# Attention with bias on one core: V loaded in place, late k side by side, 25 VectorE exponentials

## The chip, the cores and the metric

The kernel runs on one core of one Trainium2 chip. The core has five engines that work side by side: TensorE (PE in the profile) multiplies matrices into the score banks of PSUM, ScalarE (ACT) applies functions such as the exponential, VectorE (DVE) does elementwise work, GpSimd (POOL) and SyncE (SP) here mostly issue DMAs. Data comes from HBM into SBUF by DMA. The metric is the device time in microseconds of one execution; lower is better.

## The reference

Four batches of eight heads, 1024 queries and keys, head size 64, and one bias matrix for all heads:

```python
scale = 1.0 / np.sqrt(head_dim)
scores = scale * np.matmul(q, k.transpose(0, 1, 3, 2))
scores = scores + bias
scores_max = np.max(scores, axis=-1, keepdims=True)
attn = np.exp(scores - scores_max) / (np.sum(np.exp(scores - scores_max), axis=-1, keepdims=True) + 1e-8)
return np.matmul(attn, v).astype(np.float32)
```

All inputs and the output are float32. The kernel computes with bfloat16 operands and leaves out the maximum, which cancels in the quotient, and the 1e-8.

## The kernel before

The 32 heads are 16 pairs. The 1024 queries of a head are 8 chunks of 128, so there are 32 x 8 = 256 units of work, called slots: one head, one chunk of 128 queries against all 1024 keys. The scores of a slot lie in PSUM as 128 x 1024 numbers, keys along the partitions, in one of three places (two banks each, `places`).

A slot goes through these steps:

- **Fill** (`fill`, L254): eight matmuls add the scores of the slot to its place. A place keeps the bias of one chunk and goes from head to head: the operands hold the new head and the negated one before it, so that one fill takes the old scores out and puts the new ones in. Only where a place changes its chunk is the bias put in anew (`fill_half` with "b", L251).
- **Exponential** (`exp`, L268): one ScalarE activation from the place into a tile of `ep` (a ring of `NE` = 16 tiles E). The slots named in `PLAN` (23 of them) are left to VectorE, in five steps (`d_steps`, L285 to L301): `fixed` turns the scores into fixed point and so frees the place, `frac`, `inner`, `outer` and `last` make a polynomial of the fraction and write the bits of a bfloat16 number.
- **Attention step** (`av`, L318): eight matmuls multiply the E tile with V. V stands in `vall`, a ring of `VR` = 20 heads, 64 columns and a column of ones, so the row sum comes out as a 65th column. Up to seven slots share one bank.
- **Evacuation** (`evac`): VectorE takes the reciprocal of the sums (L326) and multiplies (L328) into one of three output tiles (`op`), and SyncE stores them, one DMA for each run of chunks of the same head (L739).

What feeds them: q and k of a pair are loaded by GpSimd, which also turns them to bfloat16, are transposed by TensorE (L191 with both heads side by side in 128 columns, L195 in two halves of 64 rows with `tile_position`), copied out of PSUM by VectorE (L203, L205) and doubled, for pairs from 7 on by DMAs that SyncE issues (L565). `EARLY` = 7: pairs 7 to 15 are the late ones. Their q is loaded side by side already (`beside`, L142: two DMAs of 64 numbers a run), their k as one DMA (L149) and transposed in halves. V is loaded into a landing tile (L169) and copied by VectorE into `vall` (L508). GpSimd holds its loads back: before it issues one, a copy of one number (`tick`, L483) waits until the load that stands `LATE` = 2 places before has landed.

The heads run in two groups, of 7 pairs (slots 0 to 111) and of 9 (112 to 255). In each group all heads go through three chunks, then the middle ones, then the last three, so all operands of the second group must be there between slot 112 and slot 160.

The order is written by a planner in the kernel's own Python, which runs at build time. It keeps a clock for each engine, with costs and latencies as constants (`FILL`, `BIAS`, `AV`, `EXP`, `ISSUE`, `DUE`, `LATER` and others), and picks the next instruction of each engine by due times. Two tables, `TURNS` and `D_TURNS`, overrule single decisions of TensorE and VectorE by their number. What it emits is a fixed order for each engine; on the chip, semaphores make each instruction wait for what it needs. So a late instruction holds up everything behind it on its engine.

Of the kernel before, what the change touches and what calls it, by code (L numbers as in the profile page):

```python
# [16 lines left out]
def kernel(  # L17
# [13 lines left out]
    nc = tc.nc  # L31
# [19 lines left out]
    NE = 16  # L51
# [11 lines left out]
    op = ctx.enter_context(tc.tile_pool(name="op", bufs=3))  # L63
# [20 lines left out]
    VR = 20  # L84
# [38 lines left out]
    for s, x in enumerate(slots):  # L123
# [5 lines left out]
    PLAN = (46, 52, 56, 73, 84, 87, 97, 107, 120, 128, 137, 149, 160, 167, 170, 182, 188, 194, 208, 214, 226,  # L129
            230, 240)  # L130
# [4 lines left out]
    BESIDE = (0,)  # L135
# [31 lines left out]
    def load_v(pr):  # L167
        lands[pr, "v"] = vland.tile([P, 2, NCH, D], BF, name="v16")
# [152 lines left out]
    def evac(b):  # L321
# [5 lines left out]
        ob = olast if n == 1 else op.tile([P, 7, D], F32, name="ob")  # L327
        nc.vector.tensor_tensor(ob[:, :n, :], po[:, :n, :D], rs[:, :n, :].to_broadcast([P, n, D]), op=ALU.mult)  # L328
        stores = []

        j = 0
        while j < n:
            x, c, h, start = slots[units[j]]
            i = j + 1
            while i < n and slots[units[i]][1:3] == (c + i - j, h):
                i += 1
            stores.append((of[:, h, c:c + i - j, :], ob[:, j:i, :]))
            j = i
        return stores

    with tc.manual_schedule():
# [10 lines left out]
        nc.vector.memset(sgn[D:, :], 1.0)  # L352
        nc.scalar.activation(warm[:], warm[:], ACTF.Exp)
# [19 lines left out]
        nc.vector.memset(vall[:, :, :, D:D1], 1.0)  # L373
# [65 lines left out]
        LATE, QCOST = 2, 4400  # L439
# [11 lines left out]
        LATER = 1500  # L451
# [3 lines left out]
        WINDOW = 4  # L455
# [22 lines left out]
        def issue(at, cost, depth, load, pr, *a):  # L478
# [6 lines left out]
            at = pool(at, 750)  # L485
# [4 lines left out]
        def load(pr, t):  # L490
            raw_at[pr, 1, 0] = issue(t, 1600, LATE, load_k, pr) + LATER
            raw_at[pr, 0, 0] = issue(t, QCOST, LATE, load_q, pr, slice(0, NCH)) + LATER
            for p in [pr - 1] * (pr > EARLY) + [pr] * (pr + 1 == NP):
                loads_v.append(p)
            next_v(t)

        def next_v(t):

            while loads_v and not any(x[2] // 2 == loads_v[0] - VR // 2 and y not in av_done for y, x in enumerate(slots)):
                if loads_v[0] - VL not in v_at:  # L500
                    break
                p = loads_v.pop(0)
                vland_at[p] = issue(t, 1600, LATE + (p > 12), load_v, p) + 2000
                move_v(p)

        def move_v(pr):
            def run(t2):
# [4 lines left out]

# [215 lines left out]
        def close(b, tag, t):  # L728
            units = bank[b][1]
            cost = 230 + 80 + 65 * len(units)  # L730
            last = len(av_done) >= NS - 1
# [176 lines left out]
```

## Time and profile before

| | |
|---|---|
| three runs | 230.94, 232.37, 232.49 us, median 232.37 |
| the profiled execution | 231.17 us, its span 229.2 us |
| busy share of the span: TensorE, ScalarE, VectorE, GpSimd | 96%, 95%, 86%, 28% |
| exponentials on ScalarE, slots on VectorE | 234 instructions (two of them halves), 23 |
| stores of the output, issued by SyncE | 156, and 2 by ScalarE |
| DMA packets, of these under 512 bytes | 57373, 34864 |

The span is what the profile covers; the time of the same execution also has what lies around it. The busy time of TensorE is that of pipelined matmuls with modelled ends and does not mean that it is at its peak. ScalarE's instructions overlap in part, so the time from start to start tells more than the mean duration.

### The profile page before, as it was taken

The numbers are of one execution on the slowest core, as the hardware profiler recorded it, in microseconds if no ns is written. First come the engines' busy times: TensorE is split into PE (matmuls) and PEld (weight loads), VectorE is DVE, ScalarE is ACT, GpSimd is POOL, SyncE is SP. The second block draws the span as 40 slices with busy tenths as digits, with TensorE's granted clock in tenths as the row PEclk, the third lists the DMA queues.
The fourth block names the chain that finished last, engine by engine and source line by source line (L and its number), as shares of the span: only waits on it lengthen the run. The fifth ranks groups of instructions, "written<-read, shape, count | busy, mean of one in ns | idle before, by whom it ended". The sixth has DMA issues, their size and how long they took to land.

```text
span 229.2 us, 10571 instructions
## 1 busy us (share of the span) xinstructions
PE 219.4 (96%) x4607; PEld 208.8 (91%) x4607; DVE 197.0 (86%) x301; ACT 218.1 (95%) x238; POOL 65.1 (28%) x115
## 2 busy tenths in 40 slices
PE   7899989999999999999999999999999999899992
PEld 2789989999999999999899999999999999899991
DVE  2578878629977999999999999999999999999952
ACT  3699999999999999999999999999999999999992
POOL 8816466256455443443224310000000000000000
PEclk9999999999999999999999999999999999999998
DMA  6999999989999999999899994111121102311122
GB/s 195 216 204 215 227 227 186 223 118 110 135 113 179 169 159 184 179 97 178 207 163 243 169 238 113 49 43 43 43 50 39 44 9 66 82 50 40 34 77 75
DMA packets 57373, 29.75 MB, mean 130 GB/s; under 512 B 34864, under 2 KB 53680, under 8 KB 57328
## 3 DMA queue, kind: packets, MB, share of 16 engines
q0 software_dynamic: 30336, 14.06, 49.3%
q1 hardware_dynamic: 26560, 14.40, 23.2%
q8 instruction: 36, 0.59, 1.1%
q10 hardware_dynamic: 432, 0.62, 0.9%
q14 instruction: 9, 0.07, 0.1%
HBM read 29.36 MB, written 8.39 MB: 165 GB/s over the span
## 4 chain that ended last, share of the span: by engine, by line
PE 54%; ACT 14%; DVE 12%; issue 7%; DMA 5%; SPq 5%; DVEq 0%; ACTq 0%
PE pl L254 31%; PE po L318 16%; ACT E L268 14%; SPq L739 5%; DMA out_dram<-ob 3%; PE px L191 3%; PE pl L251 2%; PE px L195 2%; DVE dy L285 2%; DMA df<-in_k_dram 2%; DVE ob L328 2%; DVE df L296 1%; DVE de L301 1%; DVE ko L203 1%; DVE side L222 1%
## 5 line engine op out<-in xcount | busy, mean ns | idle before, releaser
L268 ACT ACTIVATE E<-pl 128x1024 bf16<-128x1024 f32 (+1 forms) x234 | 215.0, 1094 | 2.3 <-PE pl L254 2.0
L318 PE MATMUL po<-vall,E 128*128 128x65 bf16 x1864 | 86.2, 194 | 1.1 <-DVE qo L205 0.4
L254 PE MATMUL pl<-qo,ko 128*128 128x128 bf16 x1024 | 77.0, 219 | 1.2 <-ACT E L268 0.6
L318 PEld LDWEIGHTS <-E 128*128 128x128 bf16 x1864 | 74.0, 98 | 2.0 <-DVE ob L328 0.6
L254 PEld LDWEIGHTS <-ko 128*128 128x128 bf16 x1160 | 69.4, 98 | 4.3 <-issue 1.4
L254 PE MATMUL pl<-qe,ke 128*128 128x128 bf16 x888 | 65.4, 219 | 0.9 <-ACT E L268 0.3
L254 PEld LDWEIGHTS <-ke 128*128 128x128 bf16 x888 | 53.2, 98 | 2.6 <-issue 0.7
L285 DVE TENSOR_SCALAR dy<-pl 128x1024 int32<-128x1024 f32 x23 | 28.0, 1218 | 1.8 <-PE pl L254 1.7
L301 DVE SCALAR_TENSOR_TENSOR de<-dy,df 128x1024 uint16<-128x1024 int32 x23 | 27.9, 1219 | 0.7 <-PE po L318 0.4
L296 DVE SCALAR_TENSOR_TENSOR df<-df 128x1024 f32<-128x1024 f32 x23 | 28.0, 1217 | 0.1
L293 DVE SCALAR_TENSOR_TENSOR df<-df 128x1024 f32<-128x1024 f32 x23 | 27.9, 1217 | 0.1
L328 DVE TENSOR_TENSOR ob<-po,rs 128x448 f32<-128x448 f32 (+4 forms) x40 | 23.3, 583 | 2.6 <-DMA out_dram<-ob 1.1
L142 POOL DMA_DIRECT2D q<-in_q_dram x18 | 16.3, 907 | 4.4 <-PE pl L254 2.7
L326 DVE RECIPROCAL rs<-po 128x7 f32<-128x7 f32 (+5 forms) x41 | 7.9, 192 | 9.9 <-PE po L318 9.8
L290 DVE TENSOR_SCALAR df<-dy 128x1024 f32<-128x1024 uint16 x23 | 15.8, 687 | 0.3
L483 POOL COPY tick<-q 1x1 bf16<-1x1 bf16 x12 | 4.4, 367 | 33.4 <-DMA q<-in_q_dram 33.4
L203 DVE COPY ko<-px 128x1024 bf16<-128x1024 bf16 (+1 forms) x16 | 10.7, 668 | 3.3 <-PE px L195 2.5
L205 DVE TENSOR_SCALAR qo<-px,sgn 128x1024 bf16<-128x1024 bf16 (+2 forms) x18 | 12.3, 683 | 1.2 <-PE px L191 1.0
L169 POOL DMA_DIRECT2D v<-in_v_dram x16 | 11.3, 707 | 2.0 <-DVE df L296 0.3
L251 PE MATMUL pl<-ident,braw 128*128 128x128 bf16 x136 | 11.3, 226 | 0.0
L149 POOL DMA_DIRECT2D k<-in_k_dram x15 | 10.7, 711 | 2.1 <-issue 0.8
L251 PEld LDWEIGHTS <-braw 128*128 128x128 bf16 x136 | 9.9, 148 | 0.0
(58 smaller groups left out, 125.4 us busy)
## 6 DMA issues: line engine op xcount, KB each, us to landing
v<-in_v_dram POOLq DMA_DIRECT2D x16, 256.0 KB, 6.6
k<-in_k_dram POOLq DMA_DIRECT2D x15, 256.0 KB, 5.5
out_dram<-ob SPq DMA_DIRECT2D x33, 96.0 KB, 3.9
out_dram<-ob SPq DMA_DIRECT2D x92, 32.0 KB, 2.6
ke<-ko SPq DMA_DIRECT2D x22, 128.0 KB, 5.5
q<-in_q_dram POOLq DMA_DIRECT2D x18, 128.0 KB, 4.7
qe<-q SPq DMA_DIRECT2D x17, 128.0 KB, 5.0
out_dram<-ob SPq DMA_DIRECT2D x31, 64.0 KB, 2.7
```

Source lines behind the costliest of these rows:

```text
L142: nc.gpsimd.dma_start(out=t[:, :, y, :], in_=(qf, kf)[x][pr][:, y].rearrange("p (c d) -> p c d", d=D))
L203: nc.vector.tensor_copy(t["ko"][:, cs, :], px[:])
L251: nc.tensor.matmul(to, braw[:, c, :].rearrange("p (kp kc) -> p kc kp", kc=NCH)[:, kc, :], ident8[:], start=i == 0, stop=False, skip_group_ ...
L254: nc.tensor.matmul(to, kk[:, kc, :], qq[:, c, :], start=False, stop=True, skip_group_check=True)
L268: nc.scalar.activation(e[:, i:i + n].rearrange("p b x -> p (b x)"), places[slots[s][0]][:, i:i + n].rearrange("p b x -> p (b x)"), ACTF.Ex ...
L285: w.tensor_scalar(t["y"][:], places[slots[s][0]].rearrange("p b x -> p (b x)"), scale * LOG2E * 65536.0, 127.0 * 65536.0, op0=ALU.mult, op ...
L290: w.tensor_scalar(t["f"][:], t["lo"], GU / 65536.0, None, op0=ALU.mult)
L293: w.scalar_tensor_tensor(t["f"][:], t["f"][:], GP, t["f"][:], op0=ALU.add, op1=ALU.mult)
L296: w.scalar_tensor_tensor(t["f"][:], t["f"][:], GQ, t["f"][:], op0=ALU.add, op1=ALU.mult)
L301: w.scalar_tensor_tensor(etile[s].bitcast(U16).rearrange("p c q -> p (c q)"), t["y"][:], 1.0 / 512.0, t["f"][:], op0=ALU.mult, op1=ALU.add)
L318: nc.tensor.matmul(po[:, j + i, :], etile[s][:, kc, :], vall[:, slots[s][2] % VR, kc, :], start=j + i + kc == 0, stop=kc == NCH - 1, skip_ ...
L328: nc.vector.tensor_tensor(ob[:, :n, :], po[:, :n, :D], rs[:, :n, :].to_broadcast([P, n, D]), op=ALU.mult)
```

## The change

- `VR` goes from 20 to 24 heads, and V of the pairs from 7 on is loaded straight into `vall` by two DMAs, one for each head, without a landing tile and without VectorE's copy.
- k of the late pairs is loaded side by side, as q is, and transposed in eight whole pieces.
- Three late loads may be in flight instead of two (`LATE`).
- 25 slots go to VectorE instead of 23, at other places (`PLAN`); the ring of E tiles has 13 tiles instead of 16.
- Stores are joined: chunks of one head or heads of one chunk at an even distance go out in one DMA (`joined`), 133 in all. There are four output tiles; only an evacuation of one unit that is closed last of all uses `olast`.
- The memset of V's ones stands earlier at the start.
- The planner has other constants, and both tables of turns are empty.

```diff
-    NE = 16
+    NE = 13
-    op = ctx.enter_context(tc.tile_pool(name="op", bufs=3))
+    op = ctx.enter_context(tc.tile_pool(name="op", bufs=4))
-    VR = 20
+    VR = 24
-    PLAN = (46, 52, 56, 73, 84, 87, 97, 107, 120, 128, 137, 149, 160, 167, 170, 182, 188, 194, 208, 214, 226,
-            230, 240)
+    PLAN = (42, 46, 54, 72, 74, 83, 90, 97, 107, 112, 135, 138, 151, 158, 161, 173, 180, 186, 194, 207, 213,
+            217, 228, 238, 246)
-    BESIDE = (0,)
+    BESIDE, INPLACE = (0, 1), 7
     def load_v(pr):
+        if pr >= INPLACE:
+            for t in range(2):
+                nc.gpsimd.dma_start(out=vall[:, (2 * pr + t) % VR, :, :D], in_=vf[pr][:, t])
+            return vall[:1, (2 * pr + 1) % VR, NCH - 1, D - 1:D]
...
+    def joined(units):
+
+        out, left = [], list(range(len(units)))
+        while left:
+            best = left[:1]
+            for j in left[1:]:
+                run, dj = [left[0], j], j - left[0]
+                dc, dh = (units[j][i] - units[left[0]][i] for i in range(2))
+                if min(dc, dh) < 0 or dc and dh:
+                    continue
+                while run[-1] + dj in left and units[run[-1] + dj] == (units[run[-1]][0] + dc, units[run[-1]][1] + dh):
+                    run.append(run[-1] + dj)
+                best = max(best, run, key=len)
+            left = [j for j in left if j not in best]
...
-    def evac(b):
+    def evac(b, last):
...
-        ob = olast if n == 1 else op.tile([P, 7, D], F32, name="ob")
+        ob = olast if n == 1 and last else op.tile([P, 7, D], F32, name="ob")
...
+        return [(to, ob[:, js]) for to, js in joined([slots[u][1:3] for u in units])]
...
+        nc.vector.memset(vall[:, :, :, D:D1], 1.0)
         nc.scalar.activation(warm[:], warm[:], ACTF.Exp)
...
-        FILL, BIAS, AV = 452, 500, 264
+        FILL, BIAS, AV = 452, 530, 264
-        ISSUE, COPY = 70, 7000
+        ISSUE, COPY = 420, 7000
-        DUE = (78, 86, 137, 98, 82, 97, 114, 84, 144)
-        t_pe, t_act, t_dve, t_pool = 9300.0, 9900.0, 9600.0, 9000
-        filled, used = {0: T0}, {0: 9900 + L_ACT}
+        DUE = (56, 89, 71, 156, 50, 70, 141, 54, 56)
+        t_pe, t_act, t_dve, t_pool = 9050.0, 9740.0, 9600.0, 9000
+        filled, used = {0: T0}, {0: 9740 + L_ACT}
-        LATE, QCOST = 2, 4400
+        LATE, COSTS = 3, {"k": 2300, "q": 2300, "v": 2300}
-        LATER = 1500
+        LATER = 1000
-        WINDOW = 4
+        WINDOW, GRACE = 4, 16
...
-            at = pool(at, 750)
+            two = pr >= EARLY and load in [load_q] * (0 in BESIDE) + [load_k] * (1 in BESIDE) or load is load_v and pr >= INPLACE
+            at = pool(at, 1500 if two else 750)
...
         def move_v(pr):
+            if pr >= INPLACE:
+                v_at[pr] = vland_at[pr] + 300
+                return
...
-            ok = [x for x in others if x[0] + x[1] <= limit]
+            ok = [x for x in others if x[0] + x[1] <= limit + GRACE]
...
-        TURNS = {9: 2, 15: 0, 25: 1, 30: 0, 49: 2, 63: 2, 64: 0, 74: 1, 93: 0, 94: 0, 98: 0, 105: 0, 109: 0,
...
-        D_TURNS = {1: 0, 25: 0, 34: 1, 39: 2, 41: 1, 42: 1, 44: 1, 66: 0, 68: 0, 70: 1, 71: 0, 76: 1, 81: 1,
...
+        TURNS = {}
+        D_TURNS = {}
```

More of the change, by code (lines that the diff above doesn't have):

```diff
@@ L490, in load @@
         def load(pr, t):
-            raw_at[pr, 1, 0] = issue(t, 1600, LATE, load_k, pr) + LATER
-            raw_at[pr, 0, 0] = issue(t, QCOST, LATE, load_q, pr, slice(0, NCH)) + LATER
+            raw_at[pr, 1, 0] = issue(t, COSTS["k"], LATE, load_k, pr) + LATER
+            raw_at[pr, 0, 0] = issue(t, COSTS["q"], LATE, load_q, pr, slice(0, NCH)) + LATER
             for p in [pr - 1] * (pr > EARLY) + [pr] * (pr + 1 == NP):
@@ L730, in close @@
             cost = 230 + 80 + 65 * len(units)
-            last = len(av_done) >= NS - 1
+            last, whole = len(av_done) >= NS - 1, len(av_done) == NS
             def run(t2):
-                stores = evac(b)
+                stores = evac(b, whole)
                 for i, (to, of_) in enumerate(stores):
```

22 lines of the change are left out of this document (7 added, 15 removed), and 3 rows, old and new, of the table TURNS.

## The prediction

> **What bounds the kernel now.** I read the busy times first, then ScalarE's timeline, because the busy times name three candidates at once:
>
> ```profile
> span 229.2 us, 10571 instructions
> ...
> PE 219.4 (96%) x4607; PEld 208.8 (91%) x4607; DVE 197.0 (86%) x301; ACT 218.1 (95%) x238; POOL 65.1 (28%) x115
> ...
> 8.22 0.60 ACT L268 ACTIVATE E<-pl 128x512 bf16<-128x512 f32 x1 [0.79 <-PE pl L254]
> ...
> 10.69 15.70 ACT L268 ACTIVATE E<-pl 128x1024 bf16<-128x1024 f32 x17
> ...
> 25.16 1.22 ACT L268 ACTIVATE E<-pl 128x1024 bf16<-128x1024 f32 x1
> ...
> 223.47 1.22 ACT L268 ACTIVATE E<-pl 128x1024 bf16<-128x1024 f32 x1
> ```
>
> The last four rows are ScalarE's timeline: start, time taken, instruction, count. The run of 17 exponentials that starts at 10.69 ends with the one at 25.16, so one starts every (25.16 - 10.69) / 16 = 0.904 us, although each lasts longer: they overlap. There are 234 (232 whole, two halves). From the one at 25.16 to the last there are 214 steps: 214 x 0.904 = 193.5 us at best, 223.47 - 25.16 = 198.3 us in fact. So ScalarE is never idle for long, and its hesitations from there on come to **4.9 us**. The last exponential ends at 223.47 + 1.22 = 224.7; 4.5 us of tail follow. The number of exponentials sets the time; all else can only add to those 4.9 us or take from them.
>
> Who makes it hesitate is read later in the run, where the other engines have no room either:
>
> ```profile
> 100.00:120.00 20.00, 19.80 (x410) 18.58 (x407) 19.01 (x28) 20.00 (x23) 5.03 (x9) 1.00 0.99 170
> 120.00:140.00 20.00, 19.90 (x435) 19.27 (x433) 19.53 (x31) 20.00 (x23) 6.18 (x11) 1.00 1.09 210
> 140.00:160.00 20.00, 19.89 (x431) 19.59 (x429) 19.66 (x25) 19.85 (x22) 0.00 (x0) 1.00 0.18 48
> ...
> sum 120.00, PE 118.41 PEld 114.70 DVE 116.15 ACT 119.75 POOL 11.21; mean PE 19.74 PEld 19.12 DVE 19.36 ACT 19.96 POOL 1.87
> ```
>
> These are busy times by stage (matmuls, weight loads, VectorE, ScalarE, GpSimd; then the granted clock, 1.00 throughout, and the DMA columns); the sum covers 100 to 220 us. VectorE is busy for 116.15 of 120 us there: 3.85 us idle. The page's 86% hides that, since it averages in a start with little VectorE work.
>
> **The change, part by part.**
>
> *25 VectorE slots in place of 23.* Two exponentials leave ScalarE: 2 x 0.904 = **-1.8 us** on the path. VectorE pays for it, with a chain of five steps a slot:
>
> ```profile
> 203.16 1.21 DVE L285 TENSOR_SCALAR dy<-pl 128x1024 int32<-128x1024 f32 x1
> 204.29 1.22 DVE L293 SCALAR_TENSOR_TENSOR df<-df 128x1024 f32<-128x1024 f32 x1
> 205.43 0.69 DVE L290 TENSOR_SCALAR df<-dy 128x1024 f32<-128x1024 uint16 x1
> 206.03 1.22 DVE L296 SCALAR_TENSOR_TENSOR df<-df 128x1024 f32<-128x1024 f32 x1
> 207.16 1.22 DVE L293 SCALAR_TENSOR_TENSOR df<-df 128x1024 f32<-128x1024 f32 x1
> ```
>
> Back to back they start 1.13, 1.14, 0.60 and 1.13 us apart, and the fifth kind (the one that writes `de`) I take at 1.13 too: 5.13 us a slot, 10.3 us for two.
>
> *V of nine late pairs in place; the tail.* In place, nine copies go:
>
> ```profile
> L508 DVE COPY vall<-v 128x1024 bf16<-128x1024 bf16 x16 | 6.9, 433 | 0.8 <-DMA v<-in_v_dram 0.8
> ...
> L203 DVE COPY ko<-px 128x1024 bf16<-128x1024 bf16 (+1 forms) x16 | 10.7, 668 | 3.3 <-PE px L195 2.5
> ...
> L228 DVE TENSOR_SCALAR q<-qo x9: 416/428/852, 69.6 to 136.9; 128x1024 bf16<-128x1024 bf16 x9
> ...
> 224.75 0.43 PE L318 MATMUL po<-vall,E 128*128 128x65 bf16 x8 [0.33 <-ACT E L268]
> ...
> 225.69 0.29 DVE L328 TENSOR_TENSOR ob<-po,rs 128x128 f32<-128x128 f32 x1 [1.06 <-DMA out_dram<-ob]
> 225.90 0.16 DVE L326 RECIPROCAL rs<-po 128x1 f32<-128x1 f32 x1
> 226.09 0.23 DVE L328 TENSOR_TENSOR olast<-po,rs 128x64 f32<-128x64 f32 x1
> ```
>
> That is 9 x 0.433 = 3.9 us of VectorE, so the engine's total grows by 6.4 us, but not evenly. Counted in the built order behind the hundredth exponential, the change has one 0.60 and three 1.13 steps more (+4.0 us), two evacuations with five units more (0.33 us each and 0.06 a unit by the last rows: +1.0), six copies of V fewer (-2.6), one copy at 0.67 and one negation at 0.43 fewer (-1.1): **+1.3 us where 3.85 are free**, in a stretch that should be 1.8 us shorter. 3.85 - 1.3 - 1.8 = 0.75 us of idle would be left. In the sum I take this at nothing; the other bound is the first rival, and past it the second.
>
> The last rows are the tail: VectorE waited 1.06 us for a store to give back one of three output tiles. With four tiles that wait goes. What is late next is the last unit's matmuls, done at 224.75 + 0.43 = 225.18, where its reciprocal started at 225.90: of the 1.06 us the path gets about **-0.6 us**. The other bound is +1: the last VectorE slot moves from 240 to 246, six slots nearer to the end, its chain (5.1 us) and an evacuation of its own (0.39 by the last two rows) then stand among the last nine exponentials (8.1 us) with five other evacuations. I keep -0.6, since the order ends the chain before the last exponential's matmuls.
>
> *k side by side.* From the chain of waits in order of time (start, time, what):
>
> ```profile
> 24.71 0.46 PE px L191 x8
> ...
> 71.84 0.52 PE po L318 x16
> ...
> 97.20 0.57 PE px L195 x16
> 97.77 0.55 PE pl L254 x8
> ...
> 98.58 0.46 PE pl L254 x8
> ...
> 148.62 0.50 PE pl L251 x8
> ```
>
> Sixteen 64-row transposes take 0.57 us and the fill behind them 0.55 where others take 0.46; eight whole ones take 0.46. That is 0.20 us a pair, 1.8 us of TensorE for nine. Does ScalarE get it? Between the 40th and the 80th exponential, the densest part of TensorE's order, stand before: 46 fills (0.46), 43 attention steps (0.26), 7 bias sets (0.50), four transposes (two at 0.66 with the slow fill, two at 0.46): 38.1 us. After: 46 fills, 45 steps, 7 bias sets, four transposes at 0.46: 38.2. ScalarE has 40 x 0.904 = 36.2. TensorE stays overbooked by 2 us, its relief spent on steps moved forward: I take nothing for it, between -1.8 and +2.
>
> *The loads.* A k or V load becomes two, with 2,048 runs of 64 numbers where 256 runs of 512 stood:
>
> ```profile
> L142 POOL DMA_DIRECT2D q<-in_q_dram x18 | 16.3, 907 | 4.4 <-PE pl L254 2.7
> ...
> L149 POOL DMA_DIRECT2D k<-in_k_dram x15 | 10.7, 711 | 2.1 <-issue 0.8
> ...
> v<-in_v_dram POOLq DMA_DIRECT2D x16, 256.0 KB, 6.6
> k<-in_k_dram POOLq DMA_DIRECT2D x15, 256.0 KB, 5.5
> ...
> q<-in_q_dram POOLq DMA_DIRECT2D x18, 128.0 KB, 4.7
> ```
>
> GpSimd's queue: 18 x (2 x 0.907 - 0.711) = +19.9 us, where it was busy 5.03 and 6.18 us of 20 and nothing is left to load at 140. Landing: q's pair, already side by side, is down 0.907 + 4.7 = 5.6 us after its first issue, k's one load after 5.5. With three in flight instead of two I take nothing. [...]
>
> GpSimd's added issues could also hold up VectorE: the negation's row above has a median of 428 ns and a longest of 852. If all nine took the longest: 9 x 0.42 = 3.8 us of VectorE; I go by the median, nothing. [...]
>
> The parts that I cost at nothing rest on these rows, of the list of waits and of VectorE's timeline:
>
> ```profile
> DVE ob L328 <- DMA out_dram<-ob: 1.1, 1, 1.1
> ...
> 1.93 0.19 DVE L373 MEMSET vall<- 128x160 bf16 x1 [0.64 <-issue]
> ...
> 5.51 0.50 DVE L376 CAST de<-dy 128x384 bf16<-128x384 f32 x1 [2.24 <-DMA dy<-in_q_dram]
> ```
>
> *Without cost:* the joined stores (133 for 158) leave SyncE's queue sooner, and the tail's is the only wait for a store in that list. 13 tiles for E instead of 16: in ten places an attention step stands within two TensorE items of the fill whose exponential needs its tile, in eleven before; if cover fails there, each costs a pair of steps, 0.52 us. The memset of V's ones moves ahead by 0.19 us of work, into the time in which VectorE waits for q. The emptied lists of turns move everything a little; only the counts above say how.
>
> **Sum:** -1.8 - 0.6 = -2.4 us. The profiled execution took 231.17 us (span 229.2 and 2.0 around it): 228.8. The median of the three runs, 232.37, lies 1.2 higher and would give 230.0. I forecast **229.5**, its own range 228 to 231.
>
> **The rivals.**
>
> *VectorE becomes the bound, the gain is given back.* If it can't work with less idle than its 3.85 us, the stretch is 1.3 us longer instead of 1.8 shorter; with the tail 231.17 + 1.3 - 0.6 = 231.9, by the median some 232.5: no change. For it: 116.15 of 120. Against: its steps can wait, only the first of a chain holds a score bank.
>
> *Slower: the first step comes late.* Until a slot's first step (L285) has read its bank, TensorE can't fill it, and ScalarE lives on two of three. It decides once VectorE's 0.75 us are used up: the first step then finds a 1.22 us step running and waits half of it. 16 late slots x 0.61 = 9.8 us: 228.8 + 9.8 = 238.6; if half of it is covered by the other banks, 233.7. I set it at 236. For it: the first steps stand in a new order throughout. Against: today's waits of this kind are inside the 4.9 us.
>
> *The late loads are late.* A load late by its 5.6 us at the second group's start stops TensorE's fixed order: 228.8 + 5.6 = 234.4. Against: of GpSimd's idle time most was spent on the landing of q, which two loads in flight enforce and three relax:
>
> ```profile
> L483 POOL COPY tick<-q 1x1 bf16<-1x1 bf16 x12 | 4.4, 367 | 33.4 <-DMA q<-in_q_dram 33.4
> ```
>
> *Faster:* the new order halves the 4.9 us: 228.8 - 2.4 = 226.4. For it: shorter transposes, no V copies that hold up a first step.
>
> **How the numbers follow.** Forecast 0.38; gain given back 0.22; slower 0.20; late loads 0.05; faster still 0.15. One per cent, 2.3 us, is what a measurement of this kernel can tell from no change: faster is below 230.0, slower above 234.7. Seven tenths of the forecast's range lie below 230.0: 0.27 + 0.15 = 0.42. Same: 0.11 + 0.22 = 0.33. Slower: 0.25. The range goes from just below the faster case, 225.5, to the slower one, 236.
>
> **What would show it.** Right: 232 exponentials 0.904 us apart, hesitations near 4.9 us, no VectorE wait for a store at the end, VectorE busy 98 to 99% from 100 to 220. The first rival shows in hesitations near 7 us with VectorE full; the second in ScalarE waiting for fills whose bank a late first step held; the third in TensorE idle before a k or q transpose, or a V step, released by a DMA. I am wrong if hesitations grow by over 2 us, or vanish.

## The result, and the profile after

The changed kernel takes 230.33 us (median of 20 runs, 229.04 to 232.64) against 232.15 us for the kernel before, measured beside it (20 runs, 230.94 to 233.52). The ratio is 0.9927, with a 95% interval of 0.9904 to 0.9951. That is 1.8 us faster by the medians and 0.7% by the ratio, which by the bound of the prediction is "within 1%", and inside the range that it gave for its own forecast (228 to 231).

The profiled execution of the changed kernel took 232.22 us, 1.9 above its median; that of the kernel before took 231.17, 1.0 below its own. So these two profiles side by side show the change as 1.1 us slower. Kept in mind, that is no obstacle: one learns from it which part of the time varies. Here is the page of the changed kernel, the row of ScalarE's exponentials (busy us, mean ns of one, idle us before them and what ended it) and three of the load rows (KB each, median us to landing) included:

```profile
span 230.4 us, 10433 instructions
...
PE 219.2 (95%) x4535; PEld 208.9 (91%) x4535; DVE 204.0 (89%) x304; ACT 216.8 (94%) x236; POOL 82.2 (36%) x133
...
DMA packets 91437, 29.74 MB, mean 129 GB/s; under 512 B 74560, under 2 KB 87744, under 8 KB 91392
...
L272 ACT ACTIVATE E<-pl 128x1024 bf16<-128x1024 f32 (+1 forms) x232 | 213.6, 1089 | 5.6 <-PE pl L258 5.5
...
k<-in_k_dram POOLq DMA_DIRECT2D x18, 128.0 KB, 5.9
q<-in_q_dram POOLq DMA_DIRECT2D x18, 128.0 KB, 6.7
vall<-in_v_dram POOLq DMA_DIRECT2D x18, 128.0 KB, 6.0
```

232 exponentials instead of 234; 74,560 packets under 512 bytes instead of 34,864. ScalarE's timeline (start, time taken, instruction, count) gives the account by the prediction's method:

```profile
24.43 2.12 ACT L272 ACTIVATE E<-pl 128x1024 bf16<-128x1024 f32 x2
...
224.48 2.06 ACT L272 ACTIVATE E<-pl 128x1024 bf16<-128x1024 f32 x2
```

Each row is two exponentials, so between the first of the one row and the first of the other lie 212 steps: 212 x 0.904 = 191.65 us at best, 224.48 - 24.43 = 200.05 in fact. The hesitations are **8.4 us**, where they were 4.9. With the same count for all profiles, in us (the start is the time at which the 20th exponential begins, the tail what follows the start of the last one):

| profile | start | steps x 0.904 | hesitations | tail | span |
|---|---|---|---|---|---|
| before | 25.16 | 193.46 | 4.86 | 5.72 | 229.2 |
| changed | 25.34 | 191.65 | 8.40 | 5.02 | 230.4 |
| changed, second profile (first experiment) | 24.97 | 191.65 | 7.02 | 5.06 | 228.7 |

Exponentials -1.8, tail -0.7, hesitations +2.2 to +3.5 (the tail is good to 0.05 us, as the span is given in tenths). By stretches, the hesitations between 40 and 80 us are 0.71 before, 2.22 and 3.54 in the two profiles after; between 80 and 110 us 0.95, then 3.14 and 0.99; behind that 2.24, then 2.68 and 2.06. All but 0.4 us of the loss lies before 110 us.

Two kinds of places make it up. The first, in TensorE's timeline (the last bracket is its idle time before the row and what ended it), and in the chain of waits:

```profile
93.64 0.44 PE L258 MATMUL pl<-qo,ko 128*128 128x128 bf16 x5 [1.52 <-issue]
...
100.66 0.58 PE L322 MATMUL po<-vall,E 128*128 128x65 bf16 x13 [1.16 <-issue]
```

```profile
91.94 0.18 PE pl L258 x3
92.12 1.52 issue
93.64 0.44 PE pl L258 x5
```

TensorE stops in the middle of a group of eight matmuls, after three of them, for 1.52 us; nothing that the profile shows released it. The second is a wait that can be read in ScalarE's and TensorE's timelines:

```profile
48.13 1.98 ACT L272 ACTIVATE E<-pl 128x1024 bf16<-128x1024 f32 x2 [0.44 <-PE pl L258]
```

```profile
45.95 0.69 PE L255 MATMUL pl<-ident,braw 128*128 128x128 bf16 x8
46.48 0.61 PE L258 MATMUL pl<-qz,ko 128*128 128x128 bf16 x8
46.92 0.67 PE L255 MATMUL pl<-ident,braw 128*128 128x128 bf16 x8
47.43 0.61 PE L258 MATMUL pl<-qz,ko 128*128 128x128 bf16 x8
```

The rows L255 put the bias in anew, eight matmuls more for a fill. Slots 42, 43 and 44 all carry bias and stand one behind the other, and slot 42 is now VectorE's: TensorE spends the time from 45.95 to 46.92 on a slot that gives ScalarE nothing, and ScalarE is dry at 48.13.

The other rows that the prediction named, in the views by stretch and of waits:

```profile
100.00:220.00 120.00, 117.42 (x2503) 114.58 (x2503) 115.65 (x149) 118.35 (x130) 14.67 (x20) 1.00 0.57 87
```

```profile
PEld L258 <- issue: 3.7, 9, 1.6
...
PE po L322 <- issue: 1.2, 1, 1.2
```

VectorE (the third time) is busy 115.65 of 120 us: 4.35 idle, not full. No row of the list has VectorE wait for a store. What it does have are weight loads and matmuls released by "issue", by nothing visible: the longest 1.6 and 1.5 us, where the kernel before has weight loads alone, the longest 0.7.

### The profile page after: what moved, and what is told of

Its sections match the earlier page's. It is cut to its first block, busy times and chain, and to the rows that moved or that the text cites. A ratio compares the mean times of both kernels' runs of the same rounds, so it can differ in the third digit from the quotient of the medians.

```text
span 230.4 us, 10433 instructions
## 1 busy us (share of the span) xinstructions
PE 219.2 (95%) x4535; PEld 208.9 (91%) x4535; DVE 204.0 (89%) x304; ACT 216.8 (94%) x236; POOL 82.2 (36%) x133
## 2 busy tenths in 40 slices
DMA packets 91437, 29.74 MB, mean 129 GB/s; under 512 B 74560, under 2 KB 87744, under 8 KB 91392
## 4 chain that ended last, share of the span: by engine, by line
PE 59%; ACT 19%; issue 9%; DVE 6%; DMA 3%; POOL 1%; SPq 1%; POOLq 0%; ACTq 0%
PE pl L258 34%; ACT E L272 19%; PE po L322 18%; PE px L195 4%; DMA braw<-in_bias_dram 3%; PE pl L255 2%; DVE dy L289 2%; PE px L199 1%; DVE ob L352 1%; DMA out_dram<-ob 1%; DVE df L297 1%; SPq L757 1%; POOL qz L371 0%; POOL qs L372 0%; DVE ke L218 0%
## 5 line engine op out<-in xcount | busy, mean ns | idle before, releaser
L322 PE MATMUL po<-vall,E 128*128 128x65 bf16 x1848 | 87.5, 194 | 2.0 <-issue 1.2
L258 PE MATMUL pl<-qo,ko 128*128 128x128 bf16 x1024 | 76.5, 219 | 2.5 <-issue 1.5
L258 PEld LDWEIGHTS <-ko 128*128 128x128 bf16 x1160 | 69.8, 98 | 5.2 <-issue 2.7
L258 PE MATMUL pl<-qe,ke 128*128 128x128 bf16 x888 | 65.9, 219 | 0.8 <-DVE dy L289 0.4
L258 PEld LDWEIGHTS <-ke 128*128 128x128 bf16 x888 | 53.2, 98 | 2.5 <-issue 1.0
L289 DVE TENSOR_SCALAR dy<-pl 128x1024 int32<-128x1024 f32 x25 | 30.5, 1219 | 3.2 <-PE pl L258 3.0
L305 DVE SCALAR_TENSOR_TENSOR de<-dy,df 128x1024 uint16<-128x1024 int32 x25 | 30.5, 1218 | 0.5 <-PE po L322 0.5
L297 DVE SCALAR_TENSOR_TENSOR df<-df 128x1024 f32<-128x1024 f32 x25 | 30.5, 1219 | 0.1
L300 DVE SCALAR_TENSOR_TENSOR df<-df 128x1024 f32<-128x1024 f32 x25 | 30.4, 1217 | 0.1
L352 DVE TENSOR_TENSOR ob<-po,rs 128x448 f32<-128x448 f32 (+5 forms) x41 | 23.5, 572 | 1.4
L294 DVE TENSOR_SCALAR df<-dy 128x1024 f32<-128x1024 uint16 x25 | 17.4, 701 | 0.1
L142 POOL DMA_DIRECT2D k<-in_k_dram x18 | 15.9, 888 | 2.9 <-PE px L195 2.0
L170 POOL DMA_DIRECT2D vall<-in_v_dram x18 | 15.8, 884 | 1.0 <-issue 0.9
L207 DVE COPY ko<-px 128x1024 bf16<-128x1024 bf16 (+1 forms) x16 | 10.7, 669 | 3.2 <-PE px L199 2.6
L255 PE MATMUL pl<-ident,braw 128*128 128x128 bf16 x136 | 11.4, 227 | 0.2 <-DMA braw<-in_bias_dram 0.2
L322 PE MATMUL po<-vall,de 128*128 128x65 bf16 x200 | 10.5, 194 | 0.2 <-DVE ob L352 0.2
L255 PEld LDWEIGHTS <-braw 128*128 128x128 bf16 x136 | 10.0, 149 | 0.4 <-DMA braw<-in_bias_dram 0.3
```

The lines of the kernel that those rows point to most:

```text
L142: nc.gpsimd.dma_start(out=t[:, :, y, :], in_=(qf, kf)[x][pr][:, y].rearrange("p (c d) -> p c d", d=D))
L170: nc.gpsimd.dma_start(out=vall[:, (2 * pr + t) % VR, :, :D], in_=vf[pr][:, t])
L255: nc.tensor.matmul(to, braw[:, c, :].rearrange("p (kp kc) -> p kc kp", kc=NCH)[:, kc, :], ident8[:], start=i == 0, stop=False, skip_group_ ...
L258: nc.tensor.matmul(to, kk[:, kc, :], qq[:, c, :], start=False, stop=True, skip_group_check=True)
L289: w.tensor_scalar(t["y"][:], places[slots[s][0]].rearrange("p b x -> p (b x)"), scale * LOG2E * 65536.0, 127.0 * 65536.0, op0=ALU.mult, op ...
L294: w.tensor_scalar(t["f"][:], t["lo"], GU / 65536.0, None, op0=ALU.mult)
```

## The experiments

Theory A: the stops without a releaser are TensorE waiting for its own instructions, whose DMA packets are late behind the late loads' many small packets. Theory C: TensorE is overbooked where VectorE's slots stand on or beside score tiles that get their bias anew. Other theories are told in the expectation that uses them. Ratios are to the kernel before, with 95% intervals; the changed kernel's is 0.9927 (0.9904 to 0.9951). In the rounds of the experiments the kernel before took 231.56 to 231.88 us, not 232.15, so a difference of medians to the 230.33 us above carries up to 0.6 us of that; the ratios do not. Except for the medians, what is said of a run is read from one profiled execution of it.

**The changed kernel again**, with nothing edited, for a second profile.

> The changed kernel itself, once more. In its first profile TensorE stood still three times in the middle of a group of eight matmuls, with no semaphore to wait for, for 1.5, 1.2 and 0.85 us, at places that are whole multiples of 256 TensorE instructions apart. Theory A (pages of instructions come late behind the loads): the stops come again, at places a multiple of 256 instructions from the old ones, and only before 140 us, while loads run; their lengths may differ. Theory B (the new order of the steps costs the time, the stops were an accident of that one execution): no such stops, and the hesitations of ScalarE without them, about 5.5 us, stay. Time 0.993 of before by both.

Measured: 230.21 us (12 runs), ratio 0.9943 (0.9908 to 0.9979). TensorE's timeline:

```profile
68.51 0.33 PE L258 MATMUL pl<-qe,ke 128*128 128x128 bf16 x3 [1.24 <-issue]
```

The stops are at 68.51, 93.54 and 129.85 us now, with TensorE idle for 1.24, 0.61 and 0.13 us; the one at 100.66 is gone. Counted in the order in which TensorE runs them, the stops of both profiles lie at its instructions 2498, 3522, 3778 and 5057, so 1024, 256 and 1279 apart: multiples of 256, to within one. The page has a queue of 35 packets for instructions (`q8 instruction: 35, 0.57, 1.1%`: 0.57 MB, so 16 KB a packet), and TensorE runs about 35 times 256 instructions, weight loads counted. That ties each packet to a boundary, and the times can be compared. In the first profile one packet starts at 90.31 and lands at 92.01; TensorE comes to its boundary at 92.12 and goes on at 93.64. The next lands at 99.14, TensorE is there at 99.51 and goes on at 100.66. In both cases TensorE goes on 1.5 to 1.6 us after the landing. The 14 profiles of this study, the two of before and after among them, have over 30 boundaries each, and they agree. At 13 boundaries TensorE's last matmul ends less than 1.2 us after the landing: at all 13 TensorE stops, for 0.27 to 1.52 us, and goes on 1.2 to 2.0 us after the landing. Where the matmul ends 1.2 to 1.6 us after it, TensorE is idle for at most 0.22 us. Where it ends later still, no stop of over 0.15 us stands that lacks another releaser; the only ones that the view puts down to "issue" are three transposes of the run with one load in flight, and each of them goes on 0.09 us after its late q or k has landed. In the kernel before, the matmul ends 1.53 us after the landing at the closest. This part of theory A the traces bear out: TensorE stopped where a packet of its instructions landed late. Whether the loads make the packets late is for the experiments below. The wait at slot 43 is the same in both profiles (0.65 and 0.64 us), which fits C.

**Two late loads in flight in the changed kernel's order.** Each late load waits on GpSimd for the load two places before instead of three; TensorE's, ScalarE's and VectorE's orders are kept.

```diff
+                late = pr >= EARLY and load in (load_k, load_q, load_v)
+                what = flight[-(depth - 1 if late else depth)][0]
```

> GpSimd holds each late load back for the load two places before it (V of the last three pairs: three) instead of three (four), as the kernel before did; the orders of TensorE, VectorE, ScalarE and SyncE stay word for word the same. Theory A: with fewer loads in flight the DMA share at 74 to 106 us falls from 1.8 towards 1.3, the stops go, some 3 us of ScalarE's hesitations with them: 227 to 228.5 us by the median, 0.98 of before. Theory B: the order is the same, so the time is, 0.993 of before. Third possibility: loads land too late for the order that was planned with three in flight; then TensorE waits before a transpose or a V step, released by a DMA, and it is slower than before.

Measured: 236.69 us, ratio 1.0215 (1.0185 to 1.0246). TensorE's timeline:

```profile
135.66 1.01 PE L195 MATMUL px<-ident,k 128*128 128x128 bf16 x8 [6.62 <-DMA k<-in_k_dram]
```

The long stops went, and ScalarE's hesitations between 80 and 110 us are 0.48 us. But the last k came 6.62 us late: the hesitations are 13.8 us in all, and those behind 110 us make up 10.7 of them. Some of that is a lower granted clock, 0.83 between 124 and 144 us: the eight transposes after the wait took 1.01 us, eight before it 0.61. So the time of this run says little of what the stops cost. It says that this order lives on three loads in flight.

**Four late loads in flight.** The same edit with `depth + 1`.

> The other way: each late load is held back for the load four places before it (V of the last three pairs: five); the other engines' orders the same. Theory A: more or longer stops between 50 and 110 us, 1 to 3 us slower than the changed kernel, 1.00 to 1.01 of before. Theory B: no change, 0.993.

Measured: 229.48 us, ratio 0.9909 (0.9886 to 0.9933): not slower than the changed kernel, as A had it, but the same or a little faster. The hesitations are 6.46 us. Stops stand at 68.44 and 129.46 alone, of 0.79 and 0.40 us. The views by stretch show why the simple form of A (more in flight, longer stops) fails; the last two columns are DMA share and GB/s, first one row of the kernel before, then the changed kernel, then this one. The DMA share is the time of all packets over that of 16 engines; it passes 1 here (1.21 to 2.17), so packets overlap.

```profile
84.00:104.00 20.00, 19.85 (x447) 19.23 (x445) 19.02 (x29) 20.00 (x23) 7.76 (x13) 1.00 1.21 161
```

```profile
64.00:84.00 20.00, 19.72 (x425) 19.52 (x423) 18.29 (x22) 19.66 (x22) 15.34 (x23) 1.00 1.80 149
84.00:104.00 20.00, 17.30 (x381) 16.76 (x379) 17.27 (x25) 17.77 (x20) 13.87 (x20) 1.00 1.88 185
```

```profile
64.00:84.00 20.00, 19.18 (x407) 18.81 (x404) 17.89 (x22) 18.75 (x21) 17.59 (x26) 1.00 2.17 163
84.00:104.00 20.00, 19.90 (x441) 19.62 (x439) 19.56 (x27) 20.00 (x23) 11.73 (x16) 1.00 1.57 174
```

The loads come earlier and denser, and are gone sooner: a share of 2.17 where TensorE is idle for 0.82 us of 20, then 1.57 where it is idle for 0.10.

**One late load in flight.** The same edit with `depth - 2`.

> Each late load waits for the one just before it (V of the last three pairs: two before); the other engines' orders the same. Both theories expect the loads to be late here: 27 late loads at about 6 us each from issue to landing take some 160 us, and q of the last pair, which the order transposes near 130 us, would land after 170. So some 20 us or more slower, with TensorE waiting for DMAs. It gives the price of loads that are late, and it shows whether page stops go when hardly anything is in flight.

Measured: 297.11 us, ratio 1.2836 (1.2803 to 1.2869), with k late by up to 20.9 us. Together with the runs before, the price of late loads in this order is 6 us at two in flight and 67 at one. It includes a lower granted clock, 0.887 on the mean of the profiled execution at one in flight.

**The late k as one load, transposed in halves**, in the changed kernel's order.

```diff
-        if pr >= EARLY and 1 in BESIDE:
-            return beside(pr, 1)
```

> k of the late pairs goes back to one load of 256 runs of 512 numbers and to sixteen 64-row transposes, as in the kernel before; everything else of the change stays, and the order of the steps on every engine too. It takes 9 x 1,792 small packets from the DMA engines and gives TensorE 1.8 us more work, of which some 0.4 us falls into its overbooked stretch. Theory A (TensorE's instruction pages come late behind small packets): the DMA share at 44 to 104 us falls from 1.8 to about 1.5, the stops become fewer, and the time stays within 1 us of the changed kernel or gains up to 1.5: 228.5 to 230.5, 0.985 to 0.995 of before. Theory B (the loads don't matter, only the order): 1 to 2 us slower than the changed kernel, 0.998 to 1.002.

Measured: 231.3 us, ratio 0.9965 (0.9936 to 0.9995). The DMA share from 44 to 104 us falls to 1.46, 1.68 and 1.40 and the longest stop without a releaser is 0.27 us, yet the kernel is 1.0 us slower than the changed one by the medians, 0.9 by the ratios (0.5 against the changed kernel's second measurement). So k side by side may be worth 0.5 to 1 us, its packets included, but the intervals overlap and the profile doesn't show where. Its hesitations, 6.37 us, are fewer than in both profiles of the changed kernel. What is longer is the start, where the 20th exponential begins at 26.29 us, and the tail, 5.46 us. The edit touches neither: the first two sets of bias took 1.06 us each instead of 0.67, and the run without bias sets below has the same slow start.

**Three output tiles.**

```diff
-    op = ctx.enter_context(tc.tile_pool(name="op", bufs=4))
+    op = ctx.enter_context(tc.tile_pool(name="op", bufs=3))
```

> Three output tiles instead of four, all else as changed, the orders too. If the fourth tile is what shortened the tail, as the prediction had it, VectorE waits for a store in the last 4 us again, by about 1 us, and the time is 0.6 us above the changed kernel: 0.996 to 0.998 of before. If the joined stores did it (four for an evacuation instead of up to six), no wait comes back and the time stays at 0.993.

Measured: 231.17 us, ratio 0.9964 (0.9936 to 0.9992). VectorE's timeline at the end, and TensorE's earlier:

```profile
226.02 0.23 DVE L352 TENSOR_TENSOR ob<-po,rs 128x64 f32<-128x64 f32 x1 [0.54 <-DMA out_dram<-ob]
```

```profile
130.17 0.45 PE L195 MATMUL px<-ident,q 128*128 128x128 bf16 x5 [1.23 <-issue]
```

The wait for a store is back, at 0.54 us, and the tail is 5.53 us instead of 5.02 and 5.06. So the fourth tile seems to be worth 0.5 us. But the run without bias sets below has four tiles and VectorE waits there for a store all the same, for 0.56 us at 223.82: four tiles don't rule the wait out, and one profile of each kind can't tell the tile from chance. Where the rest of the 0.8 us between the medians comes from isn't shown either; this profile has a stop of 1.23 us at 130.17, where the first profile of the changed kernel had 0.68 at the same boundary.

**The seven bias sets between slots 42 and 72 left out**, so the scores of seven slots and of those that follow in their places miss the right bias.

```diff
-        for what in "bs" if slots[s][3] and s > 1 else "s":
+        for what in "bs" if slots[s][3] and s > 1 and s not in (42, 43, 44, 56, 70, 71, 72) else "s":
```

> Seven of the sets of bias matmuls that change a place's chunk, those of slots 42, 43, 44, 56, 70, 71 and 72, are left out, so the scores of the middle and last chunks have a wrong bias; the order of the steps is otherwise the same. Seven sets are 3.5 us of TensorE. Theory C (between 40 and 80 us TensorE is overbooked, and a bias set in front of a VectorE slot leaves ScalarE without scores): the hesitations at 48, 58 and 72 us, 0.65 + 0.46 + 0.45 us, go and the time falls by 1.5 to 2.5 us, 0.983 to 0.987 of before. If these hesitations come from data that lands late, they stay, and so does the time.

Measured: 228.74 us (4 runs), ratio 0.987 (0.9827 to 0.9912). ScalarE's timeline:

```profile
43.12 17.56 ACT L272 ACTIVATE E<-pl 128x1024 bf16<-128x1024 f32 x19
```

```profile
84.00:104.00 20.00, 19.90 (x445) 19.58 (x443) 19.74 (x29) 20.00 (x23) 14.99 (x22) 1.00 1.90 192
```

Nineteen exponentials in one piece, where ScalarE was dry twice in the first profile of the changed kernel and three times in the second. The hesitations are 3.7 us, the lowest of all; a slow start (26.38 us) and a longer tail (5.94 us) take some 2 us of that back in this execution. The edit also takes 3.5 us of work from TensorE, so it shows that these gaps go with the bias sets, not what else they need. The DMA share stays at 1.90 (second fence, by stretch), and TensorE is idle for only 0.10 us there; its packets landed 1.6 us or more ahead of it. So a high share does not make a late packet each time.

**An order planned for two in flight.** `LATE = 2` in the planner, which then writes all orders anew.

> Two late loads in flight, as in the kernel before, but with the planner told so: it lays the order out for later landings. All other parts of the change stay. Theory A: no page stops, as with two in flight in the old order, and no load that TensorE has to wait for; 3 us of hesitations less than in the first profile of the change: 227 to 229 us, 0.98 to 0.99 of before. If three in flight is what makes the rest of the change possible, the planner must put the late transposes so late that ScalarE runs dry at the second group: slower than the changed kernel.

Measured: 240.98 us, ratio 1.0397 (1.0344 to 1.045), with hesitations of 16.3 us, 12.7 of them behind 110 us, at the late q and k. One stop of 0.42 us without a releaser is left, at 92.60. With the planner's other constants as they are, three in flight is not an extra of the change; with V and k in twice as many loads it is what makes them possible.

**Without the two slots on bias tiles.** 23 slots: 42 and 72 leave `PLAN`, and the order is planned anew.

```diff
-    PLAN = (42, 46, 54, 72, 74, 83, 90, 97, 107, 112, 135, 138, 151, 158, 161, 173, 180, 186, 194, 207, 213,
+    PLAN = (46, 54, 74, 83, 90, 97, 107, 112, 135, 138, 151, 158, 161, 173, 180, 186, 194, 207, 213,
```

> PLAN without slots 42 and 72, whose score tiles carry bias and which the changed kernel gives to VectorE: 23 slots as before the change, the rest of the changed kernel kept, the order planned anew. ScalarE then has two exponentials more, 1.8 us. Theory C (a VectorE slot on a score tile with bias makes TensorE fall behind ScalarE, because TensorE spends the time of that tile and its bias without handing ScalarE anything): the gaps of ScalarE at the slots 43 and 71 to 73, together 1.5 to 2 us in the runs of the changed kernel, shrink by 1.1 to 1.5 us, so these two slots were worth next to nothing: 0.3 to 0.7 us slower than the changed kernel, about 230.7. Rival (each slot is worth its 0.904 us wherever it lies, and the gaps belong to the bias itself): the gaps stay, 1.8 us slower than the changed kernel, about 232.1, as the kernel before. TensorE's stops for its instruction pages (theory A) are untouched by it, 1 to 2 us in either case.

Measured: 232.84 us, ratio 1.0042 (1.002 to 1.0065): 2.5 us slower than the changed kernel by the medians. It came out past the rival's number (232.1), and not by its reason. The gaps did shrink (hesitations from 40 to 80 us: 1.40 instead of 2.22 and 3.54; none at slot 43, but 0.44 at slot 56 and 0.56 at slot 71). The two exponentials cost 1.8 us, and the new order lost the rest elsewhere, behind 80 us (5.0 us against 3.1 in the second profile of the changed kernel), at a stop for one:

```profile
94.34 0.33 PE L322 MATMUL po<-vall,E 128*128 128x65 bf16 x5 [1.17 <-issue]
```

So what the slots 42 and 72 are worth by themselves isn't measured: a new plan moves everything.

**25 slots, none on a bias tile.** 41 and 62 for 42 and 72, and some later ones moved.

```diff
-    PLAN = (42, 46, 54, 72, 74, 83, 90, 97, 107, 112, 135, 138, 151, 158, 161, 173, 180, 186, 194, 207, 213,
-            217, 228, 238, 246)
+    PLAN = (41, 46, 54, 62, 74, 83, 90, 94, 107, 108, 135, 142, 151, 154, 161, 173, 178, 184, 194, 207, 213,
+            214, 226, 236, 246)
```

> 25 VectorE slots again, but none on a score tile with bias: 42 and 72 leave PLAN, 41 and 62 come in, and some of the later ones move by one to eight places; the rest as in the changed kernel. Theory C: the two exponentials stay off ScalarE and the gaps at the slots 43 and 71 to 73 shrink by 1.1 to 1.5 us: 0.8 to 1.5 us faster than the changed kernel, about 229. Rival (the gaps belong to the bias itself, wherever the slots lie): the time of the changed kernel, 230.3, with the gaps still there.

Measured: **228.85 us** (6 runs), ratio 0.9859 (0.9827 to 0.9891): faster than both kernels. ScalarE's timeline:

```profile
47.07 11.24 ACT L272 ACTIVATE E<-pl 128x1024 bf16<-128x1024 f32 x12 [0.34 <-PE pl L258]
...
71.85 3.83 ACT L272 ACTIVATE E<-pl 128x1024 bf16<-128x1024 f32 x4 [0.33 <-PE pl L258]
```

The time is what C gave, the mechanism isn't: the gaps are still there (0.53 us at slot 42, 0.57 at 71). For the first sets, slots 42 to 44, the runs fit a weaker form of C: a gap stands there with a VectorE slot on 42 or right ahead on 41, and none where the nearest is 46 (before, and the run before this one). For slots 70 to 72 they don't: 0.57 us here and 0.56 in the run before, with 74 the nearest VectorE slot, and none in the kernel before, with 73. What the four kernels have in common is that TensorE has no room there: from the start of the 40th exponential to that of the 80th it is idle for at most 0.4 us, and the stretch takes 37.1 us before, 38.4 in the changed kernel, 37.5 in the run before this one and 38.1 here. The gaps are where the excess of TensorE's work over ScalarE's 36.2 us comes out. Of the 1.5 us of span against the second profile of the changed kernel (227.2 against 228.7), 1.2 us are hesitations (5.85 against 7.02), 0.5 the tail (4.58 against 5.06), with 0.15 lost at the start. No stop of 0.4 us without a releaser stands in TensorE's timeline between 44 and 144 us. Whether the new positions of the instructions or chance keep them away, this run doesn't tell.

**The same with four in flight.**

> The edit of the run before, and four late loads in flight in place of three on GpSimd (its waits look one load further back; the order of the other engines is kept). If four in flight are a little better by themselves (229.5 against 230.3 where the slots were the change's), and the two parts do not touch each other: 0.5 us below the run before, about 228.5. If loads of many small packets make TensorE's instruction pages later (theory A in its simple form), 0.5 to 1.5 us above the run before, with stops of 0.5 us and more at distances of 256 instructions.

Measured: 229.78 us, ratio 0.9921 (0.989 to 0.9952); spans 227.5 against 227.2. No gain over the run before, perhaps 0.9 us lost by the medians. That time is inside what the simple form of A gave, but its stops are not there: the longest are 0.37 and 0.22 us, at 69.26 and 117.50. Four in flight is nothing to build on.

**V in whole rows.** Each late V load writes a head's 512 numbers of a partition in one row, so the ones and chunks are not where the product reads them.

```diff
-                nc.gpsimd.dma_start(out=vall[:, (2 * pr + t) % VR, :, :D], in_=vf[pr][:, t])
+                nc.gpsimd.dma_start(out=vall[:, (2 * pr + t) % VR].rearrange("p c d -> p (c d)")[:, :NCH * D],
+                                    in_=vf[pr][:, t].rearrange("p c d -> p (c d)"))
-            return vall[:1, (2 * pr + 1) % VR, NCH - 1, D - 1:D]
+            return vall[:1, (2 * pr + 1) % VR, NCH - 1, D - NCH:D - NCH + 1]
...
+        nc.vector.memset(vall[:, :, NCH - 1, D - NCH + 1:D], 1.0)
```

> The changed kernel with one thing different: each late V load writes a head's 512 numbers of a partition as one row of 1024 bytes at the start of the head's place in vall, not as eight rows of 64 numbers with the column of ones left free (one more small memset at the head, 0.1 to 0.3 us, for the part of a place that is then not written). Its output differs, since the ones and the chunks are not where the product with V reads them; every instruction of TensorE, ScalarE and the planner's order stays, and so do the late k loads in two halves. Theory A (TensorE's instruction pages come late behind loads of many small packets): the DMA share between 44 and 104 us falls from 1.8 to about 1.4, TensorE's stops of 0.8 us and more without a releaser go, and the time falls by 0.5 to 1.5 us, to 229 or 229.5. Rival (the stops have nothing to do with the packets, four in flight did not make them longer either): stops as before, 230.3. If late V in place costs by its landing time alone: the waits of the loading engine for V shrink and nothing else moves, 230.3 as well.

Measured: 229.61 us, ratio 0.99 (0.9858 to 0.9943). The view by stretch, and the row of the V loads:

```profile
64.00:84.00 20.00, 19.86 (x424) 19.53 (x421) 18.50 (x24) 19.52 (x22) 15.79 (x29) 1.00 1.53 157
84.00:104.00 20.00, 19.89 (x443) 19.61 (x441) 19.65 (x28) 20.00 (x23) 11.12 (x18) 1.00 1.49 187
```

```profile
vall<-in_v_dram POOLq DMA_DIRECT2D x18, 128.0 KB, 5.0
```

The share falls from 1.80 and 1.88 to 1.53 and 1.49 (from 44 to 64 us it stays at 1.78) and the landing of V from 6.0 to 5.0 us. No stop is left behind the 40th us that reaches 0.4 us, and ScalarE's hesitations between 80 and 110 us are 0.40 us, where they were 3.14 and 0.99. The wait at slot 43 stays (1.555 - 0.904 = 0.65 us). This is what A foresaw; the 0.7 us between the medians is at the lower end of what it gave, and the two intervals overlap.

All profiles together say how far the second part of A goes. Eight have three or four loads in flight and the late V and k in small packets: six of them have stops of 0.37 us or more without a releaser, two have none (no bias sets; 25 slots off the bias). Three have fewer small packets (before, k in halves, V in whole rows): none of them has a stop of over 0.27 us. That the loads make late packets likelier fits this; with one execution of each it is not shown.

## Why the prediction was right, and where it was not

The time was: 230.33 us against a forecast of 229.5 with its own range of 228 to 231, and -1.8 us against -2.4. The forecast lay on the "faster" side of its bound of 230.0, the result on the "same" side, to which it gave the smaller chance. Step by step:

- *25 slots, -1.8 us:* right. 232 exponentials, still 0.904 us apart at best.
- *The tail, -0.6:* right, -0.66 and -0.70 in the two profiles. With three tiles a wait of 0.54 us for a store came back; since a run with four tiles had one of 0.56 too, the share of the tile is likely, not shown.
- *VectorE's 1.3 us at nothing, and the first rival:* right to refuse it, and the count was right. From the 101st exponential to the last, VectorE is busy for 116.6 us before, 117.9 and 117.8 after, and idle for 6.0, 3.2 and 2.8: the 3.1 us less that I had worked out. Only the base was wrong: the 3.85 us free, from which I came to 0.75, left out the end of that stretch. In the window from 100 to 220 us VectorE is busy for 96% and 98% of the time, where I expected 98 to 99%. The hesitations behind 110 us are 2.68 and 2.06 against 2.24. The chains of 25 slots fit. The second rival fell with it: TensorE's matmuls of L258 waited 0.6 us in all for first steps. GpSimd's added issues did not cost VectorE more negations either: two of the nine are long before (745 and 852 ns, of which I had named the longest alone), one in each profile after (830 and 815). Each of the four starts during a DMA issue of GpSimd and ends 0.22 to 0.24 us after that issue; but one in the profile after, at 120.54, lies wholly within an issue and takes 426 ns. The median stays at 428 and 426.
- *k side by side at nothing (between -1.8 and +2):* inside its bounds, perhaps a gain of 0.5 to 1 us with k put back, which no profile locates.
- *The loads at nothing:* the step that failed first. I compared the landing of one load (5.6 us against 5.5; after: 5.9 to 6.7) and asked only whether loads come late. None held TensorE up in the two profiles. What they did was to raise the DMA share to 1.8 where it had been 0.96 to 1.21, and TensorE stopped, mostly 0.6 to 1.5 us at a time, where no semaphore held it and a packet of its instructions had landed late. My third rival was a late load at 5.6 us; the price was of another kind and smaller, some 2 to 3.5 us of ScalarE's hesitations in these two profiles. With V's small packets away the median was 0.7 us lower.
- *TensorE overbooked between the 40th and 80th exponential, at nothing:* the second step that failed. After, the total was right: 38.2 us worked out, and from the start of the 40th exponential to that of the 80th the changed kernel takes 38.4 us, with TensorE busy for 38.1. Before, it was not: I had 38.1 us, and the kernel takes 37.1, with TensorE busy for all but 0.1. It runs 44 fills there, one for each of the 40 exponentials and the four VectorE slots between them, where I had counted 46; after, there is one VectorE slot more, and 45 fills. So the two totals are not the same, and the change costs ScalarE 1.3 us in this stretch. They come out at the sets of bias, where ScalarE ran dry for 0.65, 0.46 and 0.45 us in the first profile. Leaving these sets out took 1.6 us off the median (1.3 by the ratio), and the hesitations from 40 to 80 us went to 1.43, of which 0.44 stand ahead of the first set.
- *Hesitations near 4.9 us:* wrong. They grew to 7.0 and 8.4 us, over the 2 us that I had named as the sign of being wrong. That the sum still held has a reason that lies outside it: the profile of before was an execution 1.0 us below its kernel's median, so that the typical growth is smaller than these profiles show. By the medians it is 2.5 - 1.8 = 0.7 us beside exponentials and tail, any gain of k's included. So the right number rests on two right terms, and on luck in the third: I took the loads and TensorE's stretch at nothing, and what they cost was small enough by the medians to stay inside the range.

What stays open: why one packet is late and another is not. The stops were gone when the V loads changed their form, but also in two runs that kept it; four loads in flight, with a share of 2.17, did not cost more than three, so the share is not the dose, and which loads stand ahead of a packet when it is asked for was not traced. How much of the best version's gain is the place of its slots and how much the missing stops was not separated either.

## What to carry to other kernels

When an engine is overbooked by a little, count its work between two hand-overs to the engine that it feeds, and count it from the trace for the kernel before as well: an item that hands over nothing still costs its share, and two fills too many on one side of the comparison hid 1.3 us here. When loads are cut into smaller pieces, look beyond their own landing time at the DMA share, and in the longest instruction stream look for idle time that no semaphore ends. And take more than one profile before costing hesitations: between two executions of one kernel they differed by 1.4 us, almost as much as the change brought.

## What the runs showed of the hardware

At 13 of the boundaries that lie 256 TensorE instructions apart TensorE stood still, for 0.27 to 1.52 us, and went on 1.2 to 2.0 us after the landing of the 16 KB packet that the count gives to that boundary; the longest stop, in the first profile of the changed kernel, came at a granted clock of 1.00. In the profiles of before and after, the packet for the next boundary starts after the last one is crossed at 66 of 71 boundaries, and at the other five at most 0.42 us before (crossed at about 86.5, the packet from 90.31 to 92.01, next boundary at 92.12). TensorE took 5.3 to 7.1 us for 256 instructions in these two profiles, stops left out. The packets that led to the 13 stops landed 4.4 to 6.1 us after the crossing (the three of the changed kernel's first profile: 5.5 to 5.6); the medians between 44 and 124 us are 3.0 before and 3.6 after.

In eight of the 14 profiles at least one crossing cost TensorE 0.27 us or more. That the loads of small packets are what delays the packet is the likely cause, not a shown one.
